# Loading the last output weights of an attention layer behind its last scores, and spreading two parts of the output sum over earlier steps

## Chip, cores and metric

One core of a Trainium2 chip runs the whole program in one launch. The metric is the device time of one execution in microseconds (us), the median of several runs.

## What is computed

A decoder trunk of two layers on 512 tokens of width 1024, all in float32. Layer A is a latent attention, layer B a sliding-window attention with 16 query heads of width 64 on 4 shared key and value heads; each layer is followed by an MLP of width 4096, and each half by a layer norm.

```python
# layer B's mixer, shortened; q: 16 heads, k and v: a band of the own and the previous block of 128
s = einsum('bnqkgd,bnjkd->bnkgqj', q, k_band) * 64 ** -0.5 + bias      # masked outside the window
m = maximum(s.max(-1), sink)
p = exp(s - m[..., None])
p = p / (p.sum(-1) + exp(sink - m))[..., None]
o = einsum('bnkgqj,bnjkd->bnqkgd', p, v_band).reshape(B, S, 1024)
x = layernorm(alpha * x + o @ w_o)
```

The place of the change is the end of this mixer: the last heads' softmax, and the product `o @ w_o`.

## The kernel before

Every float32 product is made of three matmuls of split operands. A weight chunk of 128x1024 is loaded from HBM into `raw` by a DMA on SP's queue; ACT writes its rounded high part `wh` (the function `split`, L77), and DVE or POOL subtracts to get the low part `wl` (L81). The chunks stand in one list, `stream`, in the order of their use. `weights` hands out the next chunk and prepares up to four ahead, but none from `state["hold"]` on; `prepare(n)` raises that limit by n and prepares up to it at once. A prepared chunk puts its DMA in SP's queue and its split in the queues of ACT and of DVE or POOL. The output weights of layer B are eight chunks, `w_so` 0 to 7 (`first_so` is the first of them); chunks 3, 4 and 5 are split by ACT and DVE, the other five by ACT and POOL. `fetch_two(first_so + 6, ...)` loads chunks 6 and 7 early, into a tile of their own.

Layer B's heads are run by `run_steps`. In step u it does, in this order:

- `scores(u + 2)`: eight matmuls into two PSUM banks; DVE masks, adds the bias, takes the maximum and writes `nb`; ACT takes four exponentials with their sums into `p` (`weigh`, L1440); DVE adds the sums and takes the reciprocal `ri`, and POOL multiplies `p` by it (L1449).
- fillers that are due (below).
- `turn(u)`: PE transposes `p` of head u (L1465), ACT and DVE split it into `pt` (L77, L81), and POOL multiplies it by a triangle into `pm` (L1469).
- in every second step `mix`: the value products of a pair of heads, first four matmuls into a bank `tr`, then eight into a bank `mm`. From each of the two, ACT copies a part to `low` (L1497) and DVE adds into `o` (L1499). Then ACT rounds `o` to `oh`, and POOL subtracts to `ol` (L81). `oh` and `ol` of a pair are one 128-row piece of the input of the output sum. Step 11 ends with the mix of heads 8 and 9, step 13 with heads 10 and 11, step 15 with heads 12 and 13, and heads 14 and 15 come last.

Fillers are matmul groups that PE can do while a softmax runs: first the queries of later heads and values, and from step 11 on parts of the output sum. `proj.part(t, kp)` multiplies token block t by rows 2 kp and 2 kp + 1 of the eight 128-row pieces, and adds into the block's bank: six matmuls of 128x512. So kp = 2 needs `oh` and `ol` of heads 8 to 11. A filler's entry holds its cost, the step from which it is forced, the first step in which it may run, and the function.

Matmuls, transposes and weight DMAs are kept in program order. ACT, DVE and POOL work is ordered by a scheduler at build time, which honours "behind" (one instruction may not stand ahead of another). PE, ACT, DVE, POOL and SP each run their queue in order.

```python
def weigh(h, bs, nb, sm, ri):                    # the last line of scores(h)
    for n in range(NT):
        nc.scalar.activation(p[:, n, :], bs[n // 2][:, n % 2, P:], AF.Exp, ...)       # L1440
def queue(name, ap, low=nc.vector, after=None):  # the fourth value: split behind state[after]
    ...
    with behind((state[after],) if after else None):
        state["plain"] = split(wh[:, c], wl[:, c], raw[:, c], low)
```

Of the kernel before, what the change touches and what calls it, by code (L numbers as in the profile page):

```python
# [8 lines left out]
F32 = mybir.dt.float32  # L9
# [6 lines left out]
P = 128  # L16
# [17 lines left out]
POOL_O, POOL_SO = (0, 2), (0, 1, 2, 6, 7)  # L34
# [14 lines left out]
def build(tc, nc, io, out):  # L49
    with ExitStack() as top:  # L50
        cp = top.enter_context(tc.tile_pool(name="cp", bufs=1))
        wp = top.enter_context(tc.tile_pool(name="wp", bufs=1))
        xp = top.enter_context(tc.tile_pool(name="xp", bufs=1))
# [8 lines left out]
        def nm(s):  # L62
            n_names[0] += 1
            return f"{s}_{n_names[0]}"

        def bank(cols=512, tag="mm", bufs=6):
            return ps.tile([P, cols], F32, tag=tag, bufs=bufs, name=nm(tag), padded_shape=[P, 512])
# [7 lines left out]
        def split(dst_h, dst_l, src, engine=None, keep=False):  # L75

            high = nc.scalar.activation(dst_h, src, AF.Copy)  # L77
            if keep:
                pe(high)
            with behind(state.pop("open", None)):  # L80
                low = (engine or nc.vector).tensor_sub(dst_l, src, f32(dst_h))  # L81
            if pinned[0] and engine is None:
                pe(low)
            return high, low

        def pe(ins):
            tc.keep_in_program_order(ins)
# [3 lines left out]
        def behind(pair):  # L91

            both = ExitStack()
            for ins in pair or ():
                both.enter_context(tc.issue_after(ins.ins))
            return both
# [16 lines left out]
        stream, off_ring, later, preloads = [], [], [], []  # L113
# [3 lines left out]
        def tiles_of_weights(aside=None):  # L117

            if aside:
                return aside()  # L120
            wh = wp.tile([P, 1024], F32R, tag="wh", bufs=4, name=nm("wh"))
            wl = wp.tile([P, 1024], F32R, tag="wl", bufs=4, name=nm("wl"))
            return wh, wl

        def raw_tile():
            return wp.tile([P, 1024], F32, tag="raw", bufs=2, name=nm("raw"))

        def queue(name, ap, low=nc.vector, after=None):


            index = len(stream)

            def make(pieces=1, between=None):
                cols = ap.shape[-1]
                raw = at_hand.pop(index) if index in at_hand else raw_tile()
                wh, wl = tiles_of_weights()
                for j in range(pieces):
                    c = slice(j * cols // pieces, (j + 1) * cols // pieces)
                    if between:
                        between(j)  # L140
                    if index not in fetched:
                        state["load", name] = nc.sync.dma_start(raw[:, c], ap[:, c])
                        pe(state["load", name])
                    with behind((state[after],) if after else None):
                        state["plain"] = split(wh[:, c], wl[:, c], raw[:, c], low)
                return wh, wl

            def fetch(raw):
                at_hand[index] = raw
                fetched.add(index)  # L150
                pe(nc.sync.dma_start(raw[:, : ap.shape[-1]], ap))

            fetchers[index] = fetch
            stream.append((name, make))
            off_ring.append(False)
# [128 lines left out]
        def mlp_stream(l):  # L284
            holds.append(len(stream) + 2)
            def up(q):

                return lambda r, c, jp: io["up"][
                    l, q * 8 + 4 * c + 2 * jp : q * 8 + 4 * c + 2 * jp + 2, :, r * 512 : (r + 1) * 512
                ].rearrange("c p x -> p c x")  # L290

            def down(q):
                return lambda r, c, jp: io["down"][l, q * 8 + 4 * c + 2 * (1 - r) + jp].rearrange(
                    "p (a b) -> p a b", a=2
                )

            add = {("U", q): queue_seven("up", "U", up(q)) for q in range(NFF)}
            add |= {("D", q): queue_seven("down", "D", down(q)) for q in range(NFF - 1)}
            preloads.append(add["U", 0].preload)
            for i, (which, q, n) in enumerate(steps_of()):  # L300
                if i < 2:
                    add[which, q](n, [lambda j=2 * i + jp: aside_of(j) for jp in range(2)])
                else:
                    add[which, q](n)
            for c in range(8):
                queue("down", io["down"][l, (NFF - 1) * 8 + c])
# [4 lines left out]
        first_v = len(stream)  # L311
# [3 lines left out]
            queue("w_sq", io["w_sq"][m], nc.gpsimd if m > 1 else nc.vector)  # L315
        first_so = len(stream)
        for c in range(8):
            queue("w_so", io["w_so"][c], nc.gpsimd if c in POOL_SO else nc.vector)
        mlp_stream(1)

        ready = {}
        state = {"next": 0, "at": 0, "hold": 0}
        AHEAD = 4

        def prep(i, *pieces):
            name, make = stream[i]
            ready[i] = (name, *make(*pieces))

        def prepare(n):

            state["hold"] += n
            while state["next"] < state["hold"]:
                prep(state["next"])
                state["next"] += 1
# [316 lines left out]
        def feat_major(src, w, dst, cols=slice(0, S), ks=range(KD)):  # L651
            wh, wl = w
            for k in ks:
                kc = slice(k * P, (k + 1) * P)
                group(dst, three(wh[:, kc], wl[:, kc], src.h(k, cols), src.l(k, cols)), k == 0, k == KD - 1)

        def begin(src, names, evacs, between):

            state["hold"] = first_v + 1
            ws = [weights(name) for name in names]

            def products(half_):
                late = []
                for w, evac in zip(ws, evacs):
                    cols = slice(half_ * 256, half_ * 256 + 256)
                    b = bank(256)
                    feat_major(src, w, b, cols)
                    late.append((evac, cols, b))  # L670
                return late

            late = products(0)
            for i, f in enumerate(between):
                with tc.high_priority():
                    src.turn(NT - 2 + i)
                state["hold"] = first_v + 2 if i == 0 else len(stream)
                late += f()

            with behind(src.last):  # L680
                for evac, *at in late:
                    evac(*at)
            for evac, *at in products(1):
                evac(*at)
# [275 lines left out]
        with tc.tile_pool(name="mla", bufs=1) as mp:  # L960
# [212 lines left out]
            for t, rs in ((0, (0, 1)), (1, (0, 1)), (0, (2,)), (1, (2,)), (2, range(3)), (3, range(3))):  # L1173
# [3 lines left out]
                for r in rs:  # L1177
                    wh, wl = ws[r // 2]
                    c = slice((r % 2) * 512, (r % 2 + 1) * 512)
# [94 lines left out]
            fill = []  # L1274
# [25 lines left out]
        def fetch_two(i, room):  # L1300
            for j in range(2):
                fetchers[i + j](room[:, j, :])
# [13 lines left out]
        with tc.tile_pool(name="swa", bufs=1) as mp:  # L1316
# [120 lines left out]
            def weigh(h, bs, nb, sm, ri):  # L1437
                p = mp.tile([P, NT, P], F32, tag="p", bufs=3, name=nm("p"))
                for n in range(NT):
                    nc.scalar.activation(  # L1440
                        p[:, n, :], bs[n // 2][:, n % 2, P:], AF.Exp, bias=nb[:, n : n + 1],
                        scale=SWA_SCALE, accum_out=sm[:, n : n + 1],
                    )
                own = bs[0][:, 0, NT : 2 * NT]
                nc.scalar.activation(own, nb, AF.Exp, bias=sink[:, h : h + 1])
                nc.vector.tensor_add(sm, own, sm)
                nc.vector.reciprocal(ri, sm)
                with tc.high_priority():
                    muls[h] = nc.gpsimd.tensor_mul(p, p, ri.unsqueeze(2).broadcast_to([P, NT, P]))  # L1449
                ps_of[h] = p  # L1450
# [52 lines left out]
                split(oh[m // 4][:, m % 4, :], ol[m // 4][:, m % 4, :], o.rearrange("p a b -> p (a b)"), nc.gpsimd)  # L1503

            proj = TokMajor(Pair(oh, ol), add_scaled_last, "w_so")
            fill = []
            for m in range(2, 8):
                for part in range(2):
# [2 lines left out]
                    for t in range(2, NT):  # L1511
                        fill.append((2.6, 0, -9, lambda t=t: more_values(t)))
            fill.append((0, 11, 11, preloads[1]))
            for t, kp, u in ((0, 0, 11), (0, 1, 12), (1, 0, 14), (1, 1, 14), (2, 0, 14), (2, 1, 14), (0, 2, 15), (1, 2, 16), (2, 2, 16)):
                if (t, kp) == (1, 0):
                    fill.append((0, 13, 13, lambda: fetch_two(
                        first_so + 6, xp.tile([P, 2, 1024], F32, tag="xt", bufs=8, name=nm("raw2"))
                    )))
                fill.append((1.3 if t < 2 else 0, u, u, lambda t=t, kp=kp: proj.part(t, kp)))
            begin(  # L1520
                x2, ["w_k"] * 2, [lambda cols, b, m=m: keys(m, cols, b) for m in range(2)],
# [123 lines left out]
```

## Time and profile before

| | |
|---|---|
| median of 3 runs | 991.41 us (990.88 to 992.49) |
| the profiled execution | 993.6 us, of which its span is 991.8 |
| PE busy | 981.9 us, 99% of the span |
| DVE, ACT, POOL busy | 770.5, 544.7, 238.9 us |
| mean granted TensorE clock | 0.996 |
| layer B's heads and output sum | about 541 to 651 us of the span |

The profile is of one execution. Rows of the timeline give start, duration, engine, line, operation, output and input by tile name without buffer numbers, and in brackets the idle time ahead with what ended it. Durations of matmuls overlap; the work of one is read from start to start. A line such as L105, L77 or L81 is that of a helper; the tile names tell whose work it is.

### The profile page before, as it was taken

How to read it: one execution, taken by the hardware profiler on the slowest of the kernel's cores; microseconds unless marked ns; L12 is line 12 of the kernel's file. 1: busy time of each engine (PE TensorE's matmuls, PEld its weight loads, DVE VectorE, ACT ScalarE, POOL GpSimd, SP SyncE). 2: the span in 40 equal slices, each digit the busy share in tenths (PEclk: the TensorE clock that was granted, in tenths of full speed). 3: DMA queues.
4: the chain of work that ended last, by engine and by line, in shares of the span. 5: the costliest groups of instructions: out<-in, count | busy, mean ns of one | idle time of the engine just before them, and what ended most of it. 6: DMA issues, size and time to landing. Idle time of an engine off the chain costs nothing.

```text
span 991.8 us, 15665 instructions
## 1 busy us (share of the span) xinstructions
PE 981.9 (99%) x6028; PEld 883.7 (89%) x6028; DVE 770.5 (78%) x1279; ACT 544.7 (55%) x842; POOL 238.9 (24%) x207
## 2 busy tenths in 40 slices
PE   9999999999999999999999998999999999999998
PEld 9888888998999999998898987889998998999986
DVE  6589858989768769786686787698885986898756
ACT  5557644467547547646146786436763663664620
POOL 0231101121212212210002996512121122023000
PEclk9999999999999999999999998999999999999999
DMA  7431236399779977964132223328996796898332
GB/s 262 138 95 43 89 124 199 57 221 235 139 192 233 169 166 222 228 108 147 65 107 96 86 83 141 113 58 140 279 182 120 235 213 118 222 261 146 85 128 85
DMA packets 60678, 149.54 MB, mean 151 GB/s; under 512 B 5259, under 2 KB 10300, under 8 KB 60604
## 3 DMA queue, kind: packets, MB, share of 16 engines
q0 software_dynamic: 24320, 58.73, 33.4%
q1 hardware_dynamic: 36140, 89.56, 26.0%
q8 instruction: 47, 0.77, 0.3%
q10 hardware_dynamic: 144, 0.26, 0.1%
q14 instruction: 27, 0.22, 0.1%
HBM read 146.41 MB, written 4.22 MB: 152 GB/s over the span
## 4 chain that ended last, share of the span: by engine, by line
PE 97%; DMA 1%; DVE 1%; POOL 0%; ACT 0%; issue 0%; SPq 0%; DVEq 0%; POOLq 0%
PE mm L105 89%; PE tr L105 5%; PE tr L1243 1%; DMA raw<-in_w_so 1%; PE tr L742 1%; PE tr L1465 1%; PE tr L507 0%; POOL wl L81 0%; PE tr L1007 0%; PE mm L1148 0%; ACT p L1440 0%; DVE pt L81 0%; DVE mm L1430 0%; DVE x L481 0%; ACT wh L77 0%
## 5 line engine op out<-in xcount | busy, mean ns | idle before, releaser
L105 PE MATMUL mm<-wh,fac 128*128 128x512 f32 (+1 forms) x944 | 292.5, 386 | 0.0
L77 ACT ACTIVATE wh<-wq 128x1024 fp32r<-128x1024 f32 x164 | 173.7, 1060 | 184.6 <-PE mm L105 135.7
L81 DVE TENSOR_TENSOR wl<-wq,wh 128x1024 fp32r<-128x1024 f32 x164 | 199.4, 1221 | 68.2 <-ACT wh L77 67.3
L105 PE MATMUL mm<-xth,wh 128*128 128x256 f32 (+1 forms) x928 | 243.4, 290 | 0.0
L105 PE MATMUL mm<-xth,wl 128*128 128x256 f32 (+1 forms) x800 | 233.3, 292 | 0.0
L105 PEld LDWEIGHTS mm<-wh,fac 128*128 128x128 f32 x944 | 176.3, 188 | 35.5 <-DVE fac L81 0.6
L105 PE MATMUL mm<-xtl,wh 128*128 128x256 f32 (+1 forms) x672 | 197.1, 293 | 0.0
L105 PE MATMUL mm<-wl,fac 128*128 128x512 f32 (+1 forms) x472 | 182.3, 386 | 0.0
L105 PEld LDWEIGHTS mm<-xth,wh 128*128 128x128 f32 x928 | 168.6, 192 | 3.1
L105 PEld LDWEIGHTS mm<-xth,wl 128*128 128x128 f32 x800 | 153.2, 192 | 2.7
L105 PEld LDWEIGHTS mm<-xtl,wh 128*128 128x128 f32 x672 | 128.7, 191 | 3.0
L77 ACT ACTIVATE wh<-raw 128x1024 fp32r<-128x1024 f32 (+3 forms) x86 | 84.9, 989 | 82.6 <-PE mm L105 58.3
L204 POOL DMA_DIRECT2D wq<-in_up x64 | 77.6, 1238 | 200.3 <-DVE wl L81 193.0
L105 PEld LDWEIGHTS mm<-wl,fac 128*128 128x128 f32 x472 | 88.8, 188 | 16.6
L81 DVE TENSOR_TENSOR wl<-raw,wh 128x1024 fp32r<-128x1024 f32 (+2 forms) x64 | 74.4, 1172 | 32.6 <-ACT wh L77 32.4
L204 POOL DMA_DIRECT2D wq<-in_down x48 | 42.0, 874 | 189.1 <-DVE wl L81 183.2
L81 POOL TENSOR_TENSOR wl<-raw,wh 128x1024 fp32r<-128x1024 f32 (+2 forms) x22 | 47.0, 2137 | 90.4 <-ACT wh L77 67.6
L105 PE MATMUL mm<-wh,oh 128*128 128x512 f32 x128 | 51.2, 400 | 0.0
L105 PE MATMUL mm<-wh,ol 128*128 128x512 f32 x128 | 50.6, 395 | 0.0
L105 PE MATMUL mm<-wl,oh 128*128 128x512 f32 x128 | 50.5, 394 | 0.1
L443 POOL TENSOR_TENSOR rs<-mv,half 128x1 f32<-128x1 f32 x16 | 8.8, 552 | 168.1 <-DVE mv L488 163.3
L641 DVE TENSOR_TENSOR x<-mm,x 128x512 f32<-128x512 f32 (+1 forms) x49 | 32.9, 675 | 15.4 <-PE mm L105 15.4
(246 smaller groups left out, 1790.9 us busy)
## 6 DMA issues: line engine op xcount, KB each, us to landing
wq<-in_up POOLq DMA_DIRECT2D x64, 512.0 KB, 7.2
wq<-in_down POOLq DMA_DIRECT2D x48, 512.0 KB, 7.0
wq<-in_up SPq DMA_DIRECT2D x32, 512.0 KB, 6.6
raw<-in_down SPq DMA_DIRECT2D x28, 512.0 KB, 5.7
wq<-in_down SPq DMA_DIRECT2D x24, 512.0 KB, 5.3
raw<-in_up SPq DMA_DIRECT2D x16, 512.0 KB, 4.4
raw<-in_w_o SPq DMA_DIRECT2D x8, 512.0 KB, 3.3
raw<-in_w_sq SPq DMA_DIRECT2D x8, 512.0 KB, 3.2
```

The source lines that it names most:

```text
L77: high = nc.scalar.activation(dst_h, src, AF.Copy)
L81: low = (engine or nc.vector).tensor_sub(dst_l, src, f32(dst_h))
L105: pe(nc.tensor.matmul(dst, st, mv, start=first and i == 0, stop=last and i == len(pairs) - 1, **kw))
L204: state["added", key, a, more, jp] = nc.gpsimd.dma_start(half(a, jp), chunk(*more, jp), accum_op=ALU.add)
L443: state["rs"] = nc.gpsimd.tensor_tensor(r, v, half, ALU.pow)
L641: nc.vector.tensor_add(xs[t][:, c], b, xs[t][:, c])
L742: pe(nc.tensor.transpose(pt[:, a, :], xs[t][:, k * P : (k + 1) * P], ident))
L1243: pe(nc.tensor.transpose(pt[:, kb * P : (kb + 1) * P], p[:, kb * P : (kb + 1) * P], ident))
L1465: pe(nc.tensor.transpose(pt[:, n, :], p[:, n, :], ident))
```

## The change

Layer B's output chunks are held back from chunk 3 on (`state["hold"] = first_so + 3`) until a new filler, `last_loads`, runs in step 13. It prepares chunk 3, fetches chunks 6 and 7, and then lifts the hold. Chunk 3's split may not stand ahead of the last exponential recorded by then, and step 13 has already issued `scores(15)`, the last head. The part (1, 0) of the output sum moves from step 14 to step 12, and (1, 1) from step 14 to step 13.

```diff
-            queue("w_so", io["w_so"][c], nc.gpsimd if c in POOL_SO else nc.vector)
+            queue("w_so", io["w_so"][c], nc.gpsimd if c in POOL_SO else nc.vector, "exp" if c == 3 else None)
...
-                state["hold"] = first_v + 2 if i == 0 else len(stream)
+                state["hold"] = first_v + 2 if i == 0 else first_so + 3
...
-                    nc.scalar.activation(
+                    state["exp"] = nc.scalar.activation(
                         p[:, n, :], bs[n // 2][:, n % 2, P:], AF.Exp, bias=nb[:, n : n + 1],
...
+            def last_loads():
+                prepare(1)
+                fetch_two(first_so + 6, xp.tile([P, 2, 1024], F32, tag="xt", bufs=8, name=nm("raw2")))
+                state["hold"] = len(stream)
...
-            for t, kp, u in ((0, 0, 11), (0, 1, 12), (1, 0, 14), (1, 1, 14), (2, 0, 14), (2, 1, 14), (0, 2, 15), (1, 2, 16), (2, 2, 16)):
-                if (t, kp) == (1, 0):
-                    fill.append((0, 13, 13, lambda: fetch_two(
-                        first_so + 6, xp.tile([P, 2, 1024], F32, tag="xt", bufs=8, name=nm("raw2"))
-                    )))
+            for t, kp, u in ((0, 0, 11), (0, 1, 12), (1, 0, 12), (1, 1, 13), (2, 0, 14), (2, 1, 14), (0, 2, 15), (1, 2, 16), (2, 2, 16)):
+                if (t, kp) == (1, 1):
+                    fill.append((0, 13, 13, last_loads))
```

The first place is ACT's queue around the softmax of head 12. In the rows of before, `wh_6399<-raw_6398` is the high part of chunk 3, `oh_5171<-o_6282` the rounded output of heads 6 and 7, and `p_6327` the exponentials of head 12:

```order
L77 ACTIVATE pt_6356<-tr_6358 128x4x128
L77 ACTIVATE oh_5171<-o_6282 128x512
L77 ACTIVATE wh_6399<-raw_6398 128x1024
L1398 ACTIVATE q_6351<-mm_6261 64x512
L1440 ACTIVATE p_6327,sm_6308<-mm_6310,nb_6307 128x128 x2
L1440 ACTIVATE p_6327,sm_6308<-mm_6315,nb_6307 128x128 x2
```

Of the changed kernel, the same place:

```order
L77 ACTIVATE pt_6356<-tr_6358 128x4x128
L77 ACTIVATE oh_5171<-o_6282 128x512
L1398 ACTIVATE q_6351<-mm_6261 64x512
L1440 ACTIVATE p_6327,sm_6308<-mm_6310,nb_6307 128x128 x2
L1440 ACTIVATE p_6327,sm_6308<-mm_6315,nb_6307 128x128 x2
```

Chunk 3's row has gone from here.

The second place is ACT's queue around the last exponentials. In the rows of before, `p_6515` is head 15, `low_6541`, `low_6554` and `oh_5172<-o_6535` belong to the mix of heads 10 and 11, and `pt_6586<-tr_6588` to the transposes of head 14:

```order
L1497 ACTIVATE low_6541<-tr_6536 64x512
L1440 ACTIVATE p_6515,sm_6496<-mm_6498,nb_6495 128x128 x2
L1440 ACTIVATE p_6515,sm_6496<-mm_6503,nb_6495 128x128 x2
L1445 ACTIVATE mm_6498<-nb_6495,sink 128x4
L1497 ACTIVATE low_6554<-mm_6545 64x512
L77 ACTIVATE oh_5172<-o_6535 128x512
L77 ACTIVATE pt_6586<-tr_6588 128x4x128
```

In the changed kernel head 15 is `p_6510`, chunk 3 is `wh_6520`, the mix of heads 10 and 11 is `low_6548`, `low_6561` and `o_6542`, and head 14's transposes are `tr_6582`:

```order
L1440 ACTIVATE p_6510,sm_6491<-mm_6493,nb_6490 128x128 x2
L1440 ACTIVATE p_6510,sm_6491<-mm_6498,nb_6490 128x128 x2
L77 ACTIVATE wh_6520<-raw_6519 128x1024
L1497 ACTIVATE low_6548<-tr_6543 64x512
L1445 ACTIVATE mm_6493<-nb_6490,sink 128x4
L77 ACTIVATE pt_6580<-tr_6582 128x4x128
L1497 ACTIVATE low_6561<-mm_6552 64x512
L77 ACTIVATE oh_5172<-o_6542 128x512
```

Both copies and the rounding of heads 10 and 11 now stand behind head 15's exponentials and chunk 3, and the second copy and the rounding also behind head 14's transposes.

The third place is POOL's queue at the same point. Of before (`ol_5174<-o_6535` is the low part of heads 10 and 11, `pm_6587` the triangles of heads 14 and 15):

```order
L1449 TENSOR_TENSOR p_6464<-p_6464,ri_6446 128x512
L1469 TENSOR_TENSOR pm_6486<-pt_6485,tri 128x2x3x128
L1449 TENSOR_TENSOR p_6515<-p_6515,ri_6497 128x512
L81 TENSOR_TENSOR ol_5174<-o_6535,oh_5172 128x512
L1469 TENSOR_TENSOR pm_6587<-pt_6586,tri 128x6x128 x2
```

Of the changed kernel (`ol_5174<-o_6542` and `pm_6581`):

```order
L1449 TENSOR_TENSOR p_6458<-p_6458,ri_6440 128x512
L1469 TENSOR_TENSOR pm_6481<-pt_6480,tri 128x2x3x128
L1449 TENSOR_TENSOR p_6510<-p_6510,ri_6492 128x512
L1469 TENSOR_TENSOR pm_6581<-pt_6580,tri 128x6x128
L81 TENSOR_TENSOR ol_5174<-o_6542,oh_5172 128x512
```

The low part of heads 10 and 11 now stands behind head 14's triangle. DVE's queue moved alike: chunk 3's low part stands ahead of the first add into `o_6542`, and the low part of head 14's transposes ahead of the second. On PE, between the mix of heads 10 and 11 and the transposes of head 14, there stood four parts of the output sum and now stand two. On SP, chunk 4's load moved from ahead of the loads of chunks 6 and 7 to behind them; chunk 3's stays where it was.

## Prediction

> **What bounds the kernel now.** I read the page first. PE is busy for nearly the whole span, and the chain that ended last runs on PE for nearly all of it. So a change of order can gain only where PE stands still or runs slowly.
>
> ```profile
> PE 981.9 (99%) x6028; PEld 883.7 (89%) x6028; DVE 770.5 (78%) x1279; ACT 544.7 (55%) x842; POOL 238.9 (24%) x207
> PE 97%; DMA 1%; DVE 1%; POOL 0%; ACT 0%; issue 0%; SPq 0%; DVEq 0%; POOLq 0%
> ```
>
> The 1% of DMA on that chain is the place of the change. The chain in order of time (start, length, step) shows it:
>
> ```profile
> 593.82 7.93 DMA raw<-in_w_so
> 601.80 1.06 issue
> 602.86 0.59 ACT q L1398
> 603.47 1.51 ACT p L1440 x8
> 604.99 0.04 issue
> 605.03 6.31 PE mm L105 x22
> ...
> 613.99 0.14 issue
> 614.13 0.93 PE tr L105 x4
> ```
>
> Chunk 3 of the output weights lands at 601.75. ACT has its rounding at the head of its queue, so the exponentials of head 12 stand behind it, and PE's next matmuls write the bank that those exponentials read. The rows of ACT, DVE and PE (start, duration, idle time ahead in brackets):
>
> ```profile
> 601.77 1.06 ACT L77 ACTIVATE wh<-raw 128x1024 fp32r<-128x1024 f32 x1 [2.05 <-DMA raw<-in_w_so]
> 602.86 1.22 DVE L81 TENSOR_TENSOR wl<-raw,wh 128x1024 fp32r<-128x1024 f32 x1 [1.80 <-ACT wh L77]
> 601.57 0.40 PE L105 MATMUL tr<-pm,vv 128*128 128x256 f32 x2
> 605.03 1.22 PE L105 MATMUL mm<-pt,vv 128*128 128x256 f32 x4 [3.06 <-ACT p L1440]
> 614.13 0.70 PE L105 MATMUL tr<-pt,vv 128*128 128x512 f32 x2 [0.92 <-DVE pt L81]
> ```
>
> PE stands still for 3.06 us in the mix of heads 8 and 9, and again for 0.92 at the mix of heads 10 and 11. What follows the first stall is seen in the windows (length; busy time and count of PE, PEld, DVE, ACT, POOL; then granted clock, DMA share, GB/s):
>
> ```profile
> 600.93:604.34 3.41, 1.04 (x8) 0.74 (x5) 1.58 (x6) 2.52 (x7) 1.95 (x2) 1.00 0.77 305
> 604.34:607.76 3.42, 2.73 (x13) 2.73 (x14) 2.71 (x9) 2.30 (x8) 0.00 (x0) 0.50 0.46 165
> 607.76:611.17 3.41, 3.41 (x12) 2.72 (x12) 2.83 (x16) 2.38 (x11) 2.50 (x2) 0.50 0.00 0
> 611.17:614.58 3.41, 2.49 (x19) 2.19 (x18) 2.33 (x15) 2.39 (x11) 3.07 (x4) 1.00 0.00 0
> ```
>
> The granted clock is 0.50 from 604.34 to 611.17, for 6.83 us that begin 2.4 after PE fell idle at 601.97. A stall thus costs its own length and then part of the next stretch.
>
> **The change: what it removes.** Chunk 3's rounding leaves the place ahead of head 12's exponentials. ACT was idle for 2.05 before 601.77, so from 599.72; query copy and exponentials (0.59 and 1.51) then end near 601.9, when PE is ready at 601.97. The 3.06 goes, and next late there is nothing, or 0.2 at most. Without this stall the clock has no cause to halve: 605.03 to 611.17 is 6.14 us at half rate, so 3.07 goes. The transposes that come next also need POOL's product:
>
> ```profile
> 608.67 1.04 POOL L1449 TENSOR_TENSOR p<-p,ri 128x512 f32<-128x512 f32 x1 [5.79 <-DVE nb L1434]
> ```
>
> At full rate, with the stall left in, PE would be there at 605.03 + 3.07 = 608.1, and POOL ends at 609.71. The half clock alone was therefore worth 3.07 − 1.6 = 1.5. In the changed kernel the exponentials are 3 us earlier and part (1, 0) stands ahead as cover, so I count the whole 3.07. The 0.92 wait goes too, since part (1, 1) now stands ahead of it. Removed: 3.06 + 3.07 + 0.92 = 7.05.
>
> **What it adds.** Parts (1, 0) and (1, 1) were the cover between the mix of heads 10 and 11 and the first part that needs these heads, (0, 2). And the work that makes `oh` and `ol` of these heads got longer: chunk 3 and head 14's transposes are ahead of it. The rows of before from which I build both sides:
>
> ```profile
> 615.86 0.40 PE L105 MATMUL mm<-wh,oh 128*128 128x512 f32 x1
> 616.09 0.40 PE L105 MATMUL mm<-wl,oh 128*128 128x512 f32 x1
> 621.33 0.60 PE L1465 MATMUL tr<-ident,p 128*128 128x128 f32 x4
> 621.68 0.48 PE L105 MATMUL mm<-wh,oh 128*128 128x512 f32 x1
> 615.72 0.37 ACT L1440 ACTIVATE p<-mm,nb 128x128 f32<-128x128 f32 x1
> 617.10 0.28 ACT L1445 ACTIVATE mm<-nb,sink 128x4 f32<-128x4 f32 x1
> 617.40 0.59 ACT L1497 ACTIVATE low<-mm 64x512 f32<-64x512 f32 x1
> 618.91 0.63 ACT L77 ACTIVATE oh<-o 128x512 fp32r<-128x512 f32 x1 [0.91 <-DVE o L1499]
> 622.02 0.60 ACT L77 ACTIVATE pt<-tr 128x512 fp32r<-128x512 f32 x1 [2.48 <-PE tr L1465]
> 612.27 0.30 DVE L1426 COPY_PREDICATED mm<-upper,mm 128x128 f32<-128x128 int16 x1 [0.99 <-PE mm L105]
> 614.91 0.22 DVE L1434 TENSOR_SCALAR nb<-mm,sink 128x4 f32<-128x4 f32 x1
> 615.05 0.68 DVE L81 TENSOR_TENSOR pt<-tr,pt 128x512 fp32r<-128x512 f32 x1
> 615.79 0.85 DVE L1499 TENSOR_TENSOR o<-tr,low 64x256 f32<-64x256 f32 x2
> 616.85 1.84 POOL L1469 TENSOR_TENSOR pm<-pt,tri 128x768 fp32r<-128x768 f32 x1
> 619.65 1.29 POOL L81 TENSOR_TENSOR ol<-o,oh 128x512 fp32r<-128x512 f32 x1
> ```
>
> Let T be the start of the mix of heads 10 and 11 (614.13 before). PE: the mix takes 615.86 − 614.13 = 1.73, a matmul 616.09 − 615.86 = 0.23, transposes 621.68 − 621.33 = 0.35. Twelve matmuls of parts (2, 0) and (2, 1), the transposes of head 14 and three matmuls of (0, 2) bring PE to the fourth, the first that needs the new `oh`, at T + 1.73 + 2.76 + 0.35 + 0.69 = T + 5.5.
>
> ACT and DVE: from head 15's first mask to the end of `nb` is 615.13 − 612.27 = 2.86. Part (1, 1) (1.38), the transposes and the rest of the scores (about 0.3, an estimate: the mask starts once the first of their two banks is full) lie between mask and T, with a wait of 0.4 (below) 2.4, so `nb` is there at T + 0.45. The four exponentials take 617.10 − 615.72 = 1.38, to T + 1.83; chunk 3's high part 1.06, to T + 2.9. DVE then has its low part, 1.22, to T + 4.1, and the first add, 0.85, to T + 4.95. PE ends the transposes at T + 4.85; ACT's `pt` 0.60 and second copy 0.59 run to T + 6.2, DVE's low part of them, 0.68, to T + 6.35, its second add to T + 7.2, `oh` 0.63 to T + 7.85. With a hand-over of 0.14 (the chain's row at 613.99 is one) PE waits 8.0 − 5.5 = 2.5. Then `ol`: POOL takes up head 14's triangle at T + 6.4 and ends it at T + 8.25, and `ol` at T + 9.55, while PE, with two matmuls of `oh`, would want it at T + 8.5: 1.2 more. At T itself PE waits for DVE to read head 12's transposes, whose bank it writes; DVE now has no slow stretch of PE in which to catch up, so of the 0.92 I keep 0.4 (0 to 0.92). New stalls: 0.4 + 2.5 + 1.2 = 4.1. Their bounds: each hand-over ideal and no wait at T gives 3.5, the full 0.92 and one more 0.6 ahead of `oh` gives 5.2.
>
> Does this gap halve the clock as the old one did? It is 2.5, half a us of work, then 1.2. By the windows it comes 2.4 after PE falls idle and lasts 6.83: from T + 7.9 to T + 14.7. Of that PE stands 1.3, the other 5.5 at half rate lose 2.75, of which the transposes of head 15 would have waited about 0.35 anyway. I take 2.4; bounds 0 (no halving) and 6.83 / 2 = 3.4.
>
> The moved loads: on SP's queue the rows are
>
> ```profile
> 593.82 0.88 SPq L142 DMA_DIRECT2D raw<-in_w_so  x2
> 604.11 0.33 SPq L142 DMA_DIRECT2D raw<-in_w_so  x1
> raw<-in_w_so SPq DMA_DIRECT2D x8, 512.0 KB, 5.9
> 631.38 1.05 ACT L77 ACTIVATE wh<-raw 128x1024 fp32r<-128x1024 f32 x1
> 632.93 2.08 ACT L77 ACTIVATE wh<-raw 128x1024 fp32r<-128x1024 f32 x2
> ```
>
> Chunk 3 is issued where it was and read ten us later. Chunk 4, now behind chunks 6 and 7, has until 631.38. Chunk 5 needs chunk 3's buffer, which DVE freed at 604.08 and will free near 614; 5.9 later is 620, and it is read from 632.93. If that cover were gone, each us late would be a us on PE. The two parts themselves are as long in either place: zero.
>
> Sum: −7.05 + 4.1 + 2.4 = −0.55, taken as −0.45 for the 0.1 of a late exponential at the old place. From there on PE is bound by its own matmuls and carries the shift to the end. The profiled execution, 993.6, would be 993.15; the median of the runs shown, 991.41, is 2.2 below it, and the same step gives 991.0. In this case's own range the bounds that matter are the stalls, −0.6 and +1.1, and the half clock up to +1.0; not both at their ends, so −1.4 to +1.0: 990.0 to 992.4.
>
> **Rivals.** First: the new gap leaves the clock alone. For it speaks that a matmul group splits it and that each piece (2.5, 1.2) is shorter than the 3.06 that halved it; against it, that the clock fell 2.4 into that gap. Then −7.05 + 4.1 + 0.1 = −2.85: 988.6. [...]
>
> Second: no long stall. Before, `oh` was ready at 619.54, T + 5.4, and `ol` at 620.94, T + 6.8, with exponentials ahead as well. If DVE and ACT kept that, PE would wait only 0.8 for `ol`: −7.05 + 0.4 + 0.8 = −5.85, 985.6. Against it is the order of both queues.
>
> Third, slower: most executions of before don't halve the clock in their gap, and those of the changed kernel do. What speaks for it: the profiled execution is 2.2 above the median, and the one profile can't say how often the clock falls. [...] Then the change removes only 3.06 + 1.6 + 0.92 = 5.58 (with POOL's wait in the place of the half clock) and adds 4.1 + 2.4 up to 5.2 + 3.4: +0.9 to +3.0, 992.3 to 994.4, middle 993.4. It decides where before keeps its clock more often than the changed kernel.
>
> Fourth: nothing moves, if the scheduler puts chunk 3 back ahead of head 12. The order of ACT shows that it doesn't: 991.4.
>
> **How the numbers follow.** The likeliest case gets 0.53, the first rival 0.20, the second 0.05, the third 0.20, the fourth 0.02. Predicted is 991.0. The range 988.2 to 993.6 holds the likeliest case and the first rival and half of the third, and leaves out the second and that half. A measurement of this kernel can tell about 0.2%, 2 us. Faster by more: first and second, 0.25. Slower by more: somewhat over half of the third and the upper tail of the likeliest, 0.17. Within: 0.58.
>
> **What would show it.** Right: no gap over 0.3 before the value products of heads 8 and 9, and clock 1.00 there; chunk 3's rounding straight behind the last exponentials, with no wait for a DMA; PE waiting about 2.5 for ACT's `oh` in the fourth matmul of part (0, 2), and about 1.2 for POOL's `ol` two matmuls on; and the granted clock at 0.50 behind it. Wrong: a gap for `oh` under 1 or over 4, a clock of 1.00 behind it, or a first gap that is still there with another releaser.

## The result and the profile after

The changed kernel takes 994.1 us, the median of 12 runs (992.83 to 994.84), against 991.63 of before (12 runs, 990.88 to 992.49): the ratio is 1.0025, with an interval of 1.0017 to 1.0032. It is slower by about 2.5 us, and the time lies above the range that was given. The profiled execution took 994.75 us, with a span of 993.0.

The page of the changed kernel, first the busy times and then the chain that ended last by engine:

```profile
PE 982.1 (99%) x6028; PEld 883.6 (89%) x6028; DVE 772.3 (78%) x1279; ACT 545.0 (55%) x842; POOL 239.0 (24%) x207
PE 94%; DVE 2%; ACT 1%; POOL 1%; issue 0%; DMA 0%; DVEq 0%; POOLq 0%; ACTq 0%
```

PE's work is the same, DVE's is 1.8 us more, and the chain no longer holds the DMA of the output weights: it runs through DVE, ACT and POOL instead. The rows of PE in which it waits, from 595 to 640 us:

```profile
610.18 0.70 PE L105 MATMUL tr<-pt,vv 128*128 128x512 f32 x2 [0.20 <-DVE pt L81]
619.13 0.50 PE L105 MATMUL mm<-wh,oh 128*128 128x512 f32 x1 [3.18 <-ACT oh L77]
621.34 0.80 PE L105 MATMUL mm<-wh,ol 128*128 128x512 f32 x1 [1.47 <-POOL ol L81]
```

The old gap of 3.06 us is gone and the wait of 0.92 has shrunk to 0.20, but part (0, 2) waits 3.18 for the `oh` of heads 10 and 11 and 1.47 for their `ol`. The rows behind these waits, of ACT, DVE and POOL:

```profile
611.98 1.07 ACT L77 ACTIVATE wh<-raw 128x1024 fp32r<-128x1024 f32 x1
613.09 2.77 DVE L81 TENSOR_TENSOR wl<-raw,wh 128x1024 fp32r<-128x1024 f32 x1 [1.75 <-ACT wh L77]
618.45 0.63 ACT L77 ACTIVATE oh<-o 128x512 fp32r<-128x512 f32 x1 [1.15 <-DVE o L1499]
612.92 1.85 POOL L1469 TENSOR_TENSOR pm<-pt,tri 128x768 fp32r<-128x768 f32 x1
617.26 1.04 POOL L1449 TENSOR_TENSOR p<-p,ri 128x512 f32<-128x512 f32 x1 [2.49 <-DVE ri L1447]
620.02 1.26 POOL L81 TENSOR_TENSOR ol<-o,oh 128x512 fp32r<-128x512 f32 x1
```

Chunk 3's low part on DVE took 2.77 us; in the profile of before it took 1.22. It began while POOL was in head 13's triangle, which ended at 614.77, and it ended 1.09 after that. So it stood for 1.68 us and then ran for about its usual time. POOL's product of head 15 needs `ri`, which DVE makes behind this low part: POOL stood idle for 2.49, and `ol` came after the product and one more triangle.

The windows of the changed kernel (columns as in the prediction):

```profile
613.77:617.18 3.41, 2.18 (x12) 1.50 (x10) 3.26 (x6) 1.13 (x3) 1.00 (x1) 1.00 0.13 20
617.18:620.59 3.41, 0.73 (x2) 0.30 (x2) 1.22 (x3) 0.75 (x2) 3.33 (x3) 1.00 0.36 133
620.59:624.00 3.41, 2.66 (x9) 2.29 (x10) 0.35 (x1) 0.60 (x1) 0.69 (x1) 0.50 0.03 5
624.00:627.41 3.41, 3.41 (x14) 3.10 (x13) 1.89 (x5) 1.19 (x2) 1.84 (x1) 0.50 0.00 0
627.41:630.83 3.42, 3.42 (x21) 2.98 (x20) 0.13 (x1) 1.23 (x2) 1.29 (x1) 1.00 0.00 0
```

The half rate has moved with the gap: it lasts 6.83 us as before, from 620.59.

Two theories were to be told apart, and both may be true at once. The order theory: `oh` and `ol` come too late, because chunk 3's split stands in their chain and two parts were taken from their cover. The clock theory: the profile of before shows a half rate that most executions of before have less of, so that removing it bought little, while nearly every execution of the changed kernel has it. In what follows "before" is the unchanged kernel on the same chip as the run. The first four experiments ran on one chip, where before has a median of 991.58 us (27 executions), the other four on another, where it has 992.2 (27); a time that is held against the 994.1 of the changed kernel, or against a run on the other chip, is uncertain by these 0.6.

### The profile page after: what moved, and what is told of

It reads as the page before. It is cut to its first block, busy times and chain, and to the rows that moved or that the text cites. A ratio compares the mean times of both kernels' runs of the same rounds, so it can differ in the third digit from the quotient of the medians.

```text
span 993.0 us, 15665 instructions
## 1 busy us (share of the span) xinstructions
PE 982.1 (99%) x6028; PEld 883.6 (89%) x6028; DVE 772.3 (78%) x1279; ACT 545.0 (55%) x842; POOL 239.0 (24%) x207
## 4 chain that ended last, share of the span: by engine, by line
PE 94%; DVE 2%; ACT 1%; POOL 1%; issue 0%; DMA 0%; DVEq 0%; POOLq 0%; ACTq 0%
PE mm L105 86%; PE tr L105 5%; PE tr L1243 1%; POOL wl L81 1%; PE tr L742 1%; ACT p L1440 1%; ACT wh L77 0%; PE tr L1465 0%; DMA raw<-in_w_h 0%; PE tr L507 0%; DVE o L1499 0%; POOL ol L81 0%; DVE pt L81 0%; DVE mm L1430 0%; PE tr L1007 0%
```

## The experiments

**The unchanged kernel again.** No edit.

> The unchanged kernel again, for the clock of each execution. The clock theory (the 3.06 us gap halves the clock in some executions only, while the changed kernel's longer gap does so in nearly all): the granted clock and span differ between executions by one half-rate stretch, about 0.003 and 1.5 us, and a new profile may well show the 3.06 us gap with clock 1.00 behind it and a span 1 to 2 us under 991.8. The order theory alone (the profile of before is typical, all of the loss is in the new gap): every execution at the same clock, the half-rate stretch in the profile again, span 991.8 within 0.3.

Measured: 991.69 us (990.08 to 993.13); with the executions of it that stood beside the other experiments there are 65 of the unchanged kernel. Their mean granted clocks and median times:

| granted clock | executions of before | median us | executions of the changed kernel | median us |
|---|---|---|---|---|
| 1.000 | 14 | 991.1 | 0 | |
| 0.998 | 6 | 992.2 | 0 | |
| 0.997 | 30 | 991.8 | 4 | 992.9 |
| 0.995, 0.996 | 15 | 993.2 | 8 | 994.4 |

The new profile has a span of 989.8. Its row of PE at the gap, and two windows:

```profile
604.26 0.73 PE L105 MATMUL mm<-pt,vv 128*128 128x256 f32 x4 [2.99 <-ACT p L1440]
...
600.90:604.30 3.40, 0.41 (x4) 0.21 (x2) 2.15 (x5) 3.25 (x11) 1.29 (x1) 1.00 0.58 228
605.00:608.50 3.50, 3.50 (x16) 3.26 (x16) 2.96 (x13) 2.15 (x9) 1.12 (x2) 0.53 0.29 111
```

The same gap was followed by 3.41 us of half rate here (granted clock 0.50 from 604.90 to 608.32, and 1.00 in the 3.41 on either side), not 6.83: one stretch of 3.41 and not two. A mean of 1.000 leaves no room for even one, since half of 3.41 is 0.17% of the span. Of the 65 executions of before 15 stand at the clock of the profile that the prediction was made from, and 14 show no loss of clock at all; of the 12 of the changed kernel 8 stand at that clock and none is free. At the same clock the changed kernel is slower by 994.4 − 993.2 = 1.2 and 992.9 − 991.8 = 1.1. The rest of the 2.5, about 1.3, is then that its executions lose more clock. By these medians both theories hold, with about half of the loss each.

Not all that sets the two profiles of before apart is the gap. One row of transposes ahead of it starts at 582.22 in the old profile and at 581.53 in the new one, and the mix of heads 10 and 11 behind it at 614.13 and 612.13. So 0.7 of the 2.0 is older than that row; where it arises is not shown.

**The loads alone.** Both parts back in step 14:

```diff
-for t, kp, u in (..., (1, 0, 12), (1, 1, 13), ...):
-    if (t, kp) == (1, 1):
+for t, kp, u in (..., (1, 0, 14), (1, 1, 14), ...):
+    if (t, kp) == (1, 0):
         fill.append((0, 13, 13, last_loads))
```

> Only chunk 3's split is put behind the last exponentials; parts (1, 0) and (1, 1) stay in step 14 as before. Order theory (oh and ol of heads 10 and 11 come too late because chunk 3 is ahead of them and because 12 matmuls, 2.76 us, were taken from their cover): the wait for oh falls from 3.2 to about 0.4, that for ol stays at 1 to 1.5, no half clock; some wait comes back at head 12's transposes (POOL's product, up to 1.5). 988.5 to 990.5, so 1 to 3 us under before. Rival (the chunk at that place is at fault whatever the cover): wait for oh over 2 us, time 992 or more.

Measured: 990.9 us against 991.58, ratio 0.999 (0.9981 to 0.9999), a little slower than expected. PE's only wait of more than 0.66, chunk 3's low part on DVE, and the rows of POOL around that:

```profile
609.24 1.11 PE L1465 MATMUL tr<-ident,p 128*128 128x128 f32 x4 [2.20 <-POOL p L1449]
611.87 1.23 DVE L81 TENSOR_TENSOR wl<-raw,wh 128x1024 fp32r<-128x1024 f32 x1 [2.13 <-ACT wh L77]
610.93 1.03 POOL L1449 TENSOR_TENSOR p<-p,ri 128x512 f32<-128x512 f32 x1
613.85 1.85 POOL L1469 TENSOR_TENSOR pm<-pt,tri 128x768 fp32r<-128x768 f32 x1 [1.89 <-DVE pt L81]
```

With the cover back there is no wait for `oh` or `ol` at all, so the wait of 1 to 1.5 for `ol` that I expected was wrong. In its place PE waits 2.20 at head 13's transposes, since one part fewer stands ahead of them than in the changed kernel. I had also expected no half clock, but this wait brings one, as the windows show:

```profile
605.26:608.67 3.41, 1.12 (x8) 0.74 (x6) 3.26 (x17) 2.49 (x11) 1.75 (x2) 1.00 0.00 0
608.67:612.08 3.41, 2.84 (x12) 2.65 (x13) 1.09 (x7) 3.28 (x15) 3.29 (x3) 0.50 0.00 0
```

And with POOL idle from 611.96 the low part takes 1.23.

**The parts alone.** The two steps changed, the loads as before:

> Only parts (1, 0) and (1, 1) move to steps 12 and 13; chunk 3 is split ahead of head 12's exponentials as before. Order theory: the 3.06 us gap stays; the 0.92 us wait goes; without chunk 3 (high part 1.06, low part 2.77) ahead of it oh is 2 to 3 us earlier than in the changed kernel, so PE waits 0 to 1 for oh and about 1 for ol: 991 to 993, near before. Rival (the loss is the thinner cover alone): waits for oh of about 3 and ol of 1.5 as in the changed kernel, on top of the old gap: 995 or more.

Measured: 992.4 us, ratio 1.0006 (0.9997 to 1.0015). PE's waits of more than 0.2 us:

```profile
604.77 1.16 PE L105 MATMUL mm<-pt,vv 128*128 128x256 f32 x4 [3.12 <-ACT p L1440]
620.97 0.50 PE L105 MATMUL mm<-wh,oh 128*128 128x512 f32 x1 [0.56 <-ACT oh L77]
622.32 0.50 PE L105 MATMUL mm<-wh,ol 128*128 128x512 f32 x1 [0.62 <-POOL ol L81]
```

As the order theory had it: the thin cover alone costs 0.56 and 0.62. The 3.18 of the changed kernel needs chunk 3 in the chain as well.

**Chunk 3 behind `oh`.** The changed kernel with another neighbour for chunk 3:

```diff
-                    state["exp"] = nc.scalar.activation(
+                    nc.scalar.activation(
...
-                split(oh[m // 4][:, m % 4, :], ...)
+                state["exp"] = split(oh[m // 4][:, m % 4, :], ...)[0]
...
-                if (t, kp) == (1, 1):
-                    fill.append((0, 13, 13, last_loads))
+                if (t, kp) == (2, 0):
+                    fill.append((0, 14, 14, last_loads))
```

> The changed kernel, but chunk 3's split stands behind the rounding oh of heads 10 and 11 instead of behind the last exponentials, and the loads are queued in step 14. Order theory: chunk 3's high part (1.06 us on ACT) and its low part (2.77 us on DVE, of which 1.5 is waiting out POOL's triangle) leave the chain to oh; PE's wait for oh falls from 3.2 to 0 to 0.7, that for ol is 1 to 2, no half clock: 986.5 to 989.5. Rival (the cover of 2.76 us that was taken away is what counts): wait for oh over 1.5 us and a time above 990.5.

Measured: 988.52 us (987.78 to 989.08), ratio 0.9963 (0.9949 to 0.9976): faster than both kernels. Rows of PE, DVE and POOL:

```profile
617.09 0.50 PE L105 MATMUL mm<-wh,oh 128*128 128x512 f32 x1 [0.57 <-ACT oh L77]
618.45 0.50 PE L105 MATMUL mm<-wh,ol 128*128 128x512 f32 x1 [0.62 <-POOL ol L81]
618.01 1.46 DVE L81 TENSOR_TENSOR wl<-raw,wh 128x1024 fp32r<-128x1024 f32 x1 [0.77 <-ACT wh L77]
617.11 1.28 POOL L81 TENSOR_TENSOR ol<-o,oh 128x512 fp32r<-128x512 f32 x1 [0.78 <-ACT oh L77]
618.35 2.84 POOL L1469 TENSOR_TENSOR pm<-pt,tri 128x768 fp32r<-128x768 f32 x1
```

The parts run in the same steps, the loads are queued one step later (no wait of PE ends on them), and the wait for `oh` falls from 3.18 to 0.57; no half rate follows in any of its five executions (clock 0.999 or 1.000). So, with the thin cover, it is the place of chunk 3 that costs. The low part again ends 1.08 after a POOL instruction (`ol`, over at 618.39) and takes 1.46, against 1.23 with POOL idle, and the triangle that POOL takes up meanwhile lasts 2.84 and not 1.84: here each is longer beside the other.

**A triangle in two pieces.** The changed kernel, where POOL makes head 13's triangle by two instructions:

```diff
-                    nc.gpsimd.tensor_mul(part, f32(whole[:, :, 1:]), own)
+                    for i in range(2) if h == 13 else (slice(0, 2),):
+                        nc.gpsimd.tensor_mul(part[:, i], f32(whole[:, i, 1:]), own[:, i])
```

> The changed kernel, with POOL's triangle of head 13 (1.85 us) made by two instructions of half the size. Theory (DVE's subtraction of two SBUF operands is held until the POOL instruction in progress ends, and then takes its 1.09 us): chunk 3's low part, 2.77 us in the changed kernel, falls to about 1.9 (first half of the triangle over at about 613.9 in the changed kernel's times), and the second half of the triangle starts later by about 1; PE's wait for oh falls from 3.2 to about 2.3; time 0.5 to 1 us less. Rival (the subtraction is slow there for another reason, ACT or DMA at the same buffers): 2.77 us stays, and so does the time.

Measured: 992.53 us against 994.1 of the changed kernel (the ratio to before is 1.0005, 0.9996 to 1.0013). Rows of DVE, POOL and PE:

```profile
612.75 1.93 DVE L81 TENSOR_TENSOR wl<-raw,wh 128x1024 fp32r<-128x1024 f32 x1 [1.76 <-ACT wh L77]
612.58 2.97 POOL L1470 TENSOR_TENSOR pm<-pt,tri 128x384 fp32r<-128x384 f32 x2
617.96 0.50 PE L105 MATMUL mm<-wh,oh 128*128 128x512 f32 x1 [2.34 <-ACT oh L77]
```

1.93 for an expected 1.9, and 2.34 for 2.3. DVE got in between the two pieces, and the second piece waited (2.97 for two halves of 1.85). Nothing else was touched, so the 2.77 is shown to come from POOL's instruction. The time fell by about 1.6, more than the 0.5 to 1 expected: besides the shorter wait, 5 of its 11 executions stand at a clock of 0.996, against 8 of the 12 of the changed kernel.

**Useless matmuls in the gap.** The changed kernel with 14 more matmuls ahead of part (0, 2), into a bank that nobody reads:

```diff
+            def busy():
+                b = bank()
+                wh, _ = proj.w[1]
+                group(b, [(proj.src.h(0, slice(0, P)), wh[:, 0:512])] * 14)
...
+                if (t, kp) == (0, 2):
+                    fill.append((0, 15, 15, busy))
```

> The changed kernel with 14 more matmuls of 128x512 (about 0.228 us each, 3.2 us) between head 14's transposes and part (0, 2): they do useless work, into a bank that nobody reads, in the time in which PE would wait for oh. Clock theory: the wait for oh becomes 0 to 0.3, the wait for ol stays near 1.5, the clock stays at 1.00 behind it in nearly all executions, and the kernel with more work is faster: 991 to 992.5. Rival (the half rate has another cause, or costs nothing since others wait anyway): 994 to 995, like the changed kernel.

Measured: 991.43 us (991.1 to 992.04); all of its 11 executions have a clock of 0.999 or 1.000. PE's rows and the windows of the gap:

```profile
614.24 3.70 PE L105 MATMUL mm<-wh,oh 128*128 128x512 f32 x15
620.58 0.50 PE L105 MATMUL mm<-wh,ol 128*128 128x512 f32 x1 [1.50 <-POOL ol L81]
...
616.40:619.80 3.40, 2.68 (x11) 1.61 (x9) 1.21 (x3) 0.74 (x2) 3.33 (x3) 1.00 0.33 129
619.80:623.20 3.40, 2.62 (x18) 2.46 (x19) 0.88 (x2) 1.20 (x2) 0.97 (x2) 1.00 0.00 0
```

The kernel with more work is 2.7 us faster than the changed kernel, with `oh` no earlier (it ends 8.9 us after the start of the mix in both) and `ol` still waited for by 1.50. The difference is the half rate behind the gap. From the matmul that waits for `ol` to the first one behind the next mix PE takes 627.39 − 620.58 = 6.81 here, and 630.92 − 621.34 = 9.58 in the changed kernel, 2.77 more. These are the second ends:

```profile
627.39 0.40 PE L105 MATMUL mm<-wh,oh 128*128 128x512 f32 x1
...
630.92 0.40 PE L105 MATMUL mm<-wh,oh 128*128 128x512 f32 x1
```

Keeping PE busy was enough to prevent it.

**One part back as cover,** in the version with chunk 3 behind `oh`: `(1, 1, 13)` becomes `(1, 1, 14)`.

> Like the version with chunk 3 behind oh, but part (1, 1) goes back to step 14, as cover for oh and ol (1.38 us). Expected: the waits of 0.57 for oh and 0.62 for ol go, the wait at the mix of heads 10 and 11 grows from 0.20 to 0.6 to 1.5; 987.3 to 988.8. If the cover were the main thing: 987.4 or less; if the wait at the mix takes it all back: 988.5 or more.

Measured: 988.51 us, ratio 0.9964 (0.9951 to 0.9978), the same as with the part in step 13: the wait at the mix takes all of it back.

```profile
608.55 0.66 PE L1465 MATMUL tr<-ident,p 128*128 128x128 f32 x4 [0.33 <-POOL p L1449]
610.22 0.71 PE L105 MATMUL tr<-pt,vv 128*128 128x512 f32 x2 [1.02 <-DVE pt L81]
618.78 0.73 PE L105 MATMUL tr<-pt,vv 128*128 128x512 f32 x2 [0.29 <-DVE pt L81]
```

The waits for `oh` and `ol` went, and 1.02 and 0.33 came in at the mix and the transposes ahead of it: cover that is moved is missing where it stood.

**Chunk 3 behind `oh`, both parts in step 14,** so that only the loads differ from before:

> Chunk 3 behind oh and both parts back in step 14, so only the loads differ from before. By the run with the loads alone (waits of 2.20 us for POOL's product at head 13's transposes and 0.66 for DVE, none for oh or ol) chunk 3's place between exponentials and oh costs nothing once the cover is there: 990.3 to 991.3, the same as that run. Rival (chunk 3 ahead of oh costs by itself): 989 or less.

Measured: 990.86 us, ratio 0.9985 (0.9976 to 0.9993), the same as the loads alone.

```profile
609.88 0.66 PE L1465 MATMUL tr<-ident,p 128*128 128x128 f32 x4 [2.20 <-POOL p L1449]
```

With full cover the place of chunk 3 makes no difference. So neither the place nor the thin cover is dear alone; together they are. Four versions show it: loads alone 990.9, parts alone 992.4, both with chunk 3 ahead of `oh` 994.1, both with chunk 3 behind `oh` 988.5.

## Why the prediction was wrong, point by point

**What the change removes** was right: the 3.06 and all but 0.20 of the 0.92 are gone, and chunk 3's split waits for no DMA. T, the start of the mix of heads 10 and 11, came at 610.18; by the sum it is 614.13 − 3.06 − 3.07 − 0.52, and 2.76 later for the two parts that now stand ahead of it: 610.24. The moved loads cost PE nothing. Every sign that was named for being right came too, and the waits were only longer. None of them tested the step that failed.

**The step that failed: carrying one execution's half rate over to the median.** The sum took 3.07 for the half clock out of the profile of before and then put "the same step" on a median 2.2 us lower. That difference was the warning: the profiled execution, at 993.6, has 6.83 us of half rate, and only 15 of the 65 executions of before stand at its clock. The others had less to lose. In the changed kernel the median lies only 0.65 below the profiled execution, not 2.2, so 1.5 of the 3.1 between 991.0 and 994.1 come from this step. The other 1.6 is the sum itself: from one profiled execution to the other it has −0.45, and 1.15 was measured. That alone would not have left the range: 991.4 + 1.15 is 992.6.

The failed step was written down as the third rival, at 0.20 and with a middle of 993.4. The 994.1 lies in its span, of which the part above 993.6 lay outside the range. Its condition was too strong, though: not most of the executions of before, but 14 of 65, show no loss of clock. Another 36 stand at 0.997 or 0.998, and the one profile of them shows half the stretch.

**Mis-sized: chunk 3's low part.** T was 610.18 in the profile. `nb`, the exponentials and the high part came as worked out (T + 2.87 for a predicted T + 2.9). The low part ended at T + 5.7, not T + 4.1, because of POOL's triangle; `oh` at T + 8.9 for T + 7.85; PE waited 3.18 for 2.5. The price could have been read: in the profile of before, chunk 5's low part begins while POOL makes `ol`, which ends at 634.83, and ends 1.09 after it. The rows of DVE and POOL:

```profile
634.01 1.91 DVE L81 TENSOR_TENSOR wl<-raw,wh 128x1024 fp32r<-128x1024 f32 x1 [0.33 <-ACT wh L77]
633.10 1.73 POOL L81 TENSOR_TENSOR ol<-o,oh 128x512 fp32r<-128x512 f32 x1 [3.38 <-ACT oh L77]
```

I took the one row of chunk 3 itself, 1.22, which happened to begin 0.02 us before a POOL instruction ended. I left the work beside it out: with a POOL instruction going on, the low part took 1.91, 2.77, 1.93 and 1.46 in these traces, against 1.23 with POOL idle from 611.96 on (the loads alone).

**Mis-sized too: POOL's queue ahead of `ol`.** I had the triangle taken up at T + 6.4. The product of head 15 was still ahead of it, waiting for `ri` behind that low part; `ol` ended at T + 11.1, not T + 9.55, and PE waited 1.47 for 1.2. Waits in all: 4.85 for 4.1.

**The half clock of the new gap** came, for 6.83 us as assumed, but from 620.59, some 2.5 later than by the fixed delay that I took from one row. It cost 2.77 by the run with the useless matmuls, where the sum has 2.4. The first rival (no halving) is out: none of the 12 executions kept the full clock. The second (no long stall) is out by the 3.18, and the fourth (nothing moves) by the order of ACT.

Of the sum's own 1.6, the waits are 0.75 and the half clock 0.4. The remaining half a us I can't place in single rows; it stays open.

## What to carry to other kernels

Moving work forward takes cover away from where it stood: before giving it up, write out the chain that this cover hides, with all that the change itself adds to it, and put the added work behind the chain's last instruction rather than in its middle (988.5 against 994.1 here). For the duration of an instruction take rows with the same neighbour on POOL, not the one row at its old place (1.22 there and 2.77 at the new place here). And when a profile's own time lies away from the median of the runs, find out which of its terms is not typical before subtracting it.

## What the hardware showed

By the traces' clock records the full rate ahead of the gap lasted 597.332 us in the profile of before and 614.399 in that of the changed kernel, and the half rate behind it 6.827 in both: 175, 180 and twice 2 times 3.4133. With the two triangles the half rate lasted 6.82; in the other four profiles that have it (the repeat, the loads alone, the parts alone, chunk 3 behind `oh` with both parts in step 14) it lasted 3.41 or 3.42, one such length.

In all seven PE was idle for 2.20 to 3.12 us of the last 3.41 ahead of the half rate, also where no single gap was longer than 2.20 (the loads alone, with 2.29 from two gaps). Two places with less idling show a clock of 1.00 behind it: the gap of 1.50 with the useless matmuls, and the stretch from 613.77 to 617.18 of the changed kernel, with 1.23. Of the first 3.41 us of half rate PE was idle for 0.69, 0.75 and 1.43 in the three profiles where a second such stretch followed, and for 0.57 or nothing in the four where none did. What happens between these figures no run shows.

Where the change of the clock falls against the program differs between executions: in the first profile of before the rate halves 2.37 us into the gap that begins at 601.97, and in the repeat 0.64 us after the gap from 601.27 to 604.26 is over. That this is also what spares the executions without any loss is a guess of mine; no profile of one was taken.
